# A fourth double-width raw weight tile in the wide layers of a two-layer encoder

## The chip, the cores and the metric

The kernel runs on one core of one Trainium2 chip. The metric is the time of one execution in microseconds (us), measured on the device; of several runs the median is taken. The core has five engines that matter here: TensorE (PE in the profile; PEld is its weight load), VectorE (DVE), ScalarE (ACT), GpSimd (POOL), and SyncE (SP), which here only issues transfers. Each engine works through its own queue in order and waits on semaphores that other engines and transfers raise.

## The reference

What is computed is the trunk of a bidirectional encoder with two layers over 512 tokens of width 1024, in float32:

```python
for layer in range(DEPTH):
    hn = rmsnorm(h, norm_mix[layer])
    if layer % 2 == 0:
        h = h + hybrid_attention(hn, ...)
    else:
        h = h + neighbourhood_attention(hn, ...)
    h = h + sq_relu_mlp(rmsnorm(h, norm_ffn[layer]), ffn_w_up[layer], ffn_w_down[layer])
return rmsnorm(h, final_norm)

def sq_relu_mlp(h, w_up, w_down):
    u = jax.nn.relu(h @ w_up)
    return (u * u) @ w_down
```

`w_up` is 1024 x 4096 and `w_down` 4096 x 1024. Layer 0 has 16 heads of full attention over the 512 tokens, layer 1 has 16 heads of attention over a window.

## The kernel before

Activations lie transposed (features on partitions, tokens along the free dimension). Every product is made in three matmuls from split operands: a value is its rounded high half (`hi`, made by ACT) and the rest (`lo`, made by DVE as value minus `hi`); high x high, high x low and low x high are summed in PSUM.

The MLP of each layer (`mlp_swept`) has four parts. First 6 tiles of 128 hidden features are made by plain products (`plain`), and their share of the second product is added. Then comes the **wide stage**, 26 more tiles in 13 blocks of 256 features: here a product of 2 x 2 tiles is made from seven block products instead of eight (`Seven`, in the manner of Strassen and Winograd), which needs sums of weight blocks. Then the **sweeps** multiply 22 of these tiles by `w_down` in the same manner in three kinds of passes of 11 steps, with weight sums prepared beforehand in DRAM (`SumsAhead`, transfers issued by ACT and POOL, L819 and L828). The last 4 tiles are plain again.

In the wide stage a block has 4 chunks (`seven_chunk`). Two chunks share one **raw pair**, a tile of 128 x 2048 floats from `raw_pair`: two transfers of 256 KB by SP (L312) fill four of the eight blocks of each half, POOL makes the others in three operations (L315 to L317), ACT makes `hi` of a half (L322) and DVE `lo` (L323). A pair can be loaded anew when both halves have been split. There are three such tiles (`bufs=3`), and three `hi` and three `lo` tiles. A chunk is used by 21 matmuls of 128x256 (L402 to L404). After four chunks a block's four PSUM banks are emptied by ACT (L411) and DVE (L412 to L415), and `raw_evac` squares the relu on ACT (L1210, L1211).

`weights(i)` is called ahead of the matmuls of chunk i. It asks for the loads of all chunks up to i + LOAD, with LOAD = 5, and for the splits up to i + AHEAD, with AHEAD = 2. The same tiles and the same function serve every other weight in the kernel; `raw_half` gives out one half of a pair at a time, from the list `spare`.

The order of instructions on each engine is set by a planner when the kernel is built: the program's order is the priority, and an instruction that could start earlier by the planner's own costs is pulled forward. Only the attention of layer 1 has an order written out by hand (`fixed_order`), and single instructions are held in program order by `keep_in_program_order`. Dependences are found by the planner from the parts of a tile that each instruction touches.

The pool `pp` has five tiles of 128 x 512 floats. They hold the attentions' probabilities (`p`, written at L1061 and L1698), the accumulator of the norms' squares (`acc`, L547), and in the third kind of sweeps one operand of each step (`u`, split at L1376 and L1377). The pool `scp` has six scratch tiles of the same size.

In layer 0 the kernel also prepares bias rows for layer 1's attention (`bias_rows`, L1285 to L1305) by SP transfers and POOL copies while the MLP runs.

Of the kernel before, what the change touches and what calls it, by code (L numbers as in the profile page):

```python
# [8 lines left out]
F32 = mybir.dt.float32  # L9
F32R = mybir.dt.float32r  # L10
# [6 lines left out]
S = 512  # L17
D = 1024
P = 128
# [11 lines left out]
def f32(ap):  # L31
    return ap.bitcast(F32)
# [3 lines left out]
def encoder_kernel(ctx: ExitStack, tc: tile.TileContext, ins, out, dbg=None):  # L36
# [3 lines left out]
    big = ctx.enter_context(tc.tile_pool(name="big", bufs=1))  # L40
    wp = ctx.enter_context(tc.tile_pool(name="wp", bufs=3))
    scp = ctx.enter_context(tc.tile_pool(name="scp", bufs=6))
    pp = ctx.enter_context(tc.tile_pool(name="pp", bufs=5))
    tp = ctx.enter_context(tc.tile_pool(name="tp", bufs=6))
    ps = ctx.enter_context(tc.tile_pool(name="ps", bufs=1, space=PSUM))
    dr = ctx.enter_context(tc.tile_pool(name="dr", bufs=1, space=bass.MemoryType.DRAM))
# [14 lines left out]
    def nm(s):  # L61
        cnt[0] += 1
        return f"{s}_{cnt[0]}"
# [18 lines left out]
    def sbk():  # L82
        return bank("s", 2)

    def stb():
        return bank("t", 2)

    def ob():
        return bank("o", 1)

    def scratch(dt=F32):
        return scp.tile([P, 512], dt, tag="sc", name=nm("sc"))

    def tiny(n, dt=F32):
        return tp.tile([P, n], dt, tag=f"ti{n}", name=nm("ti"))

    def keep(shape, dt, name):
        return big.tile(shape, dt, tag=name, name=name)


    cst = keep([P, C_ROPE], F32, "cst")
    ident = cst[:, C_ID : C_ID + P]
# [78 lines left out]


    spare = []

    def raw_pair():
        return wp.tile([P, 2048], F32, tag="raw", bufs=3, name=nm("raw"))

    def raw_half():
# [50 lines left out]


    asked, loaded, ready, low_parts = [], [], [], []
    AHEAD, LOAD = 2, 5

    def plan(*spec, make=None):
        asked.append((make or chunk, spec))
        return len(asked) - 1

    def weights(i, ahead=AHEAD):
        while len(loaded) < min(i + LOAD + 1, len(asked)):
            make, spec = asked[len(loaded)]  # L250
            loaded.append(make(*spec))
            next(loaded[-1])
        while len(ready) < min(i + ahead + 1, len(asked)):
            hi, lo, lows = next(loaded[len(ready)])
            ready.append((hi, lo))
            low_parts.append(lows)

            give_low(len(ready) - fixed[0])
        give_low(i + 1)
        return ready[i]  # L260
# [4 lines left out]
    def give_low(n):  # L265
        while given[0] < n:
            for z in low_parts[given[0]]:
                z()
            given[0] += 1
# [247 lines left out]
    def tick(us):  # L517
        if beat["rest"]:
            return
        beat["left"] -= us  # L520
        if beat["left"] <= 0:
            beat["left"] += beat["every"]
            next(beat["work"], None)

    def drain():
        for _ in beat["work"]:
            pass
# [33 lines left out]


    X = [Slot() for _ in range(KD)]
    acc = pp.tile([P, S], F32, tag="p", name=nm("acc"))

    def make_x(k):
        b = stb()
# [453 lines left out]
    def attend(heads, step):  # L1021


        late_t, late_v = [], []

        def transpose(h, i, p):
            if i % 2 == 0:
                h["pt"] = Slot(), Slot()
            h3, l3 = (s_.t.rearrange("p (k q) -> p k q", k=4)[:, :, (i % 2) * P : (i % 2 + 1) * P] for s_ in h["pt"])
            tb = stb()  # L1030
            for k in range(4):
                PE.transpose(tb[:, k * P : (k + 1) * P], p[:, k * P : (k + 1) * P], ident)  # L1032
            t3 = tb.rearrange("p (k q) -> p k q", k=4)
            ACT.activation(h3, t3, AF.Copy)
            DVE.tensor_tensor(l3, t3, f32(h3), op=ALU.subtract)
            if i % 2:
                late_v.append((h, i // 2, h["pt"]))

        def values(h, half, pt):
            if half == 0:  # L1040
                h["o"] = ob()
            o = h["o"]
            for k in range(4):
                for n, m in enumerate(pt):
                    PE.matmul(o[:, 256 * half : 256 * half + 256], h["vlhs"](k), m.t[:, 256 * k : 256 * k + 256],  # L1045
                              start=k == 0 and n == 0, stop=k == 3 and n == 1, skip_group_check=True)
            for s_ in pt:
                s_.free()
            if half:
                fold(o, h["e"])  # L1050
                h["after"]()

        def scores(h, i):
            s = sbk()
            pl = h["passes"](i)
            for n, (lh, rh) in enumerate(pl):
                PE.matmul(s, lh, rh, start=n == 0, stop=n == len(pl) - 1)  # L1057
            h["done"](i)
            t = tiny(4)
            p = pp.tile([P, 512], F32, tag="p", name=nm("p"))  # L1060
            DVE.tensor_tensor_reduce(p, s, zeros.to_broadcast([P, S]), op0=ALU.add, op1=ALU.min, scale=h["scale"](i),  # L1061
                                     scalar=3e38, accum_out=t[:, 1:2])
            ACT.activation(p, p, AF.Exp, bias=t[:, 1:2], scale=-1.0, accum_out=t[:, 2:3])
            DVE.reciprocal(t[:, 3:4], t[:, 2:3])  # L1064
            POOL.tensor_scalar(p, p, t[:, 3:4], 1.0, op0=ALU.mult, op1=ALU.mult)  # L1065
            return p

        for h in heads:
            for i in range(4):
                ripe = list(late_v)  # L1070
                tick(1.3)
                p = scores(h, i)
                if len(late_t) == 3:
                    transpose(*late_t.pop(0))
                late_t.append((h, i, p))
                if ripe:
                    values(*late_v.pop(0))
                step(h, i)
        for x in late_t:
            transpose(*x)  # L1080
            while late_v:
                values(*late_v.pop(0))
            fill.run(1.5)
# [88 lines left out]
    def first_product(l):  # L1172

        w = ins["ffn_w_up"][l]
        X = [Slot() for _ in range(KD)]
        acc = pp.tile([P, S], F32, tag="p", name=nm("acc"))
        for k in range(KD):
            split_g(hT[:, k, :], gffn(l, k), X[k].pair())
            sumsq_acc(k, acc, DVE)
# [160 lines left out]
    class Sweeps:  # L1340
# [28 lines left out]
        def tokens(self, kind, kp):  # L1369

            r, s2 = self.parts(kp)
            two = Slot()
            d = two.t.rearrange("p (q z n) -> p q z n", q=2, z=2)

            def split_to(hi, lo, src):
                ACT.activation(hi, src, AF.Copy)  # L1376
                DVE.tensor_tensor(lo, src, f32(hi), op=ALU.subtract)  # L1377

            got = [d[:, 0], d[:, 1]]
            if kind == 0:  # L1380
                split_to(d[:, :, 0], d[:, :, 1], r[:, 0:4:2])
                self.one(kp)
                if kp < 2:
                    self.two(kp)
            elif kind == 1:
                for q, src in enumerate((r[:, 0], s2)):
                    split_to(d[:, q, 0], d[:, q, 1], src)
                if kp + 2 < self.n:
                    self.two(kp + 2)
                if kp + 2 >= self.n:  # L1390
                    self.three(kp + 2 - self.n)
                    self.four(kp + 2 - self.n)
            else:
                if kp + 2 < self.n:
                    self.three(kp + 2)
                    self.four(kp + 2)
                split_to(d[:, :, 0], d[:, :, 1], r[:, 1:3])
                one = pp.tile([P, 512], F32R, tag="p", name=nm("u"))
                e = one.rearrange("p (z n) -> p z n", z=2)
                split_to(e[:, 0], e[:, 1], r[:, 3])  # L1400
                got.append(e)
                self.R[kp].free()
                if kp % 4 == 3 or kp == self.n - 1:
                    self.second[kp // 4].free()
            return two, got
# [90 lines left out]

    def mlp_swept(l, made, last=None):

        stage, ahead, later = first_product(l)
        w = ins["ffn_w_down"][l]  # L1500
        bias = bias_rows() if l == 0 else iter(())
# [29 lines left out]

        rest = split_more()
        drain()
        reserve[0] = 6
        if last:
            beside = last(FIRST + RAW, V)
# [22 lines left out]


    X = [Slot() for _ in range(KD)]
    acc = pp.tile([P, S], F32, tag="p", name=nm("acc"))
    for k in range(KD):
        split_g(hT[:, k, :], gmix(1, k), X[k].pair())
    XP = [s_.pair() for s_ in X]
# [103 lines left out]
    def attend_C(step):  # L1669
# [18 lines left out]

        def scores(h, us):
            sb = sbk()  # L1690
            pt = pp.tile([P, 512], F32, tag="p", name=nm("p"))
            got = []
            for n, u in enumerate(us):
                unit(h, u, sb[:, 256 * n : 256 * n + 256], n == 0)
            for n, u in enumerate(us):
                tt = tiny(4)
                h[u] = pt[:, 256 * n : 256 * n + 256]
                DVE.tensor_tensor_reduce(h[u], sb[:, 256 * n : 256 * n + 256], h["bias"][:, 0 if u < 3 else 1, :],  # L1698
                                         op0=ALU.add, op1=ALU.min, scale=-1.0, scalar=3e38, accum_out=tt[:, 0:1])
                got.append((h[u], tt))  # L1700
            return got
# [290 lines left out]
```

## Time and profile before

| | us |
|---|---|
| median of 3 runs | 1185.34 |
| lowest and highest of them | 1185.12, 1186.34 |
| the profiled execution | 1187.7 |
| its span, first to last instruction | 1185.9 |
| wide stage of layer 0 | 338.4 to 476.3 |
| wide stage of layer 1 | 903.4 to 1039.2 |
| mean granted TensorE clock | 0.997 of full speed |

The page of the profile shows one execution. The groups of the wide stage in it are these (line, engine, operation, tiles, shapes and count; busy us and mean ns of one; idle time of the engine just before them and what ended most of it):

```profile
L323 DVE TENSOR_TENSOR wlo<-raw,whi 128x896 fp32r<-128x896 f32 x104 | 151.3, 1467 | 63.9 <-ACT whi L322 63.6
L322 ACT ACTIVATE whi<-raw 128x896 fp32r<-128x896 f32 x104 | 95.8, 946 | 98.7 <-POOL raw L317 44.7
L315 POOL TENSOR_TENSOR raw<-raw 128x256 f32<-128x256 f32 x52 | 56.0, 1078 | 76.3 <-DMA raw<-in_ffn_w_up_dram 56.4
L316 POOL TENSOR_TENSOR raw<-raw 128x512 f32<-128x512 f32 x52 | 83.1, 1599 | 4.1
L317 POOL TENSOR_TENSOR raw<-raw 128x256 f32<-128x256 f32 x52 | 68.0, 1308 | 4.1
```

Idle time of an engine that is not the bound costs nothing by itself; what counts is whether it reaches TensorE. A matmul's end is modelled, and matmuls overlap, so a matmul's busy time is longer than its share of the pipeline: the count of matmuls in a stretch says more than their busy time. A wait is put down to the engine whose signal came last.

### The profile page before, as it was taken

How to read it: one execution, taken by the hardware profiler on the slowest of the kernel's cores; microseconds unless marked ns; L12 is line 12 of the kernel's file. 1: busy time of each engine (PE TensorE's matmuls, PEld its weight loads, DVE VectorE, ACT ScalarE, POOL GpSimd, SP SyncE). 2: the span in 40 equal slices, each digit the busy share in tenths (PEclk: the TensorE clock that was granted, in tenths of full speed). 3: DMA queues.
4: the chain of work that ended last, by engine and by line, in shares of the span. 5: the costliest groups of instructions: out<-in, count | busy, mean ns of one | idle time of the engine just before them, and what ended most of it. 6: DMA issues, size and time to landing. Idle time of an engine off the chain costs nothing.

```text
span 1185.9 us, 20854 instructions
## 1 busy us (share of the span) xinstructions
PE 1152.0 (97%) x7596; PEld 1034.0 (87%) x7596; DVE 917.2 (77%) x1617; ACT 668.1 (56%) x1147; POOL 459.4 (39%) x486
## 2 busy tenths in 40 slices
PE   9989999999999999999999999999999999999997
PEld 8667778888899899999988998988889989999995
DVE  4788888778968777998474676767996777899855
ACT  5468576664535556756253565655553555576625
POOL 3267353333478795000001243333265878700000
PEclk9999999999999999999999999999999999999999
DMA  7123467654656666877345577778557666575702
GB/s 270 54 76 85 116 148 197 180 103 133 147 147 175 164 143 171 272 236 250 131 119 148 141 215 183 207 175 214 166 112 192 161 174 160 150 243 170 257 2 71
DMA packets 129543, 191.55 MB, mean 162 GB/s; under 512 B 12659, under 2 KB 81184, under 8 KB 128736
## 3 DMA queue, kind: packets, MB, share of 16 engines
q1 hardware_dynamic: 112304, 136.61, 36.8%
q0 software_dynamic: 14976, 29.38, 15.5%
q10 hardware_dynamic: 2160, 24.22, 6.3%
q8 instruction: 60, 0.98, 0.4%
q14 instruction: 43, 0.35, 0.1%
HBM read 167.75 MB, written 52.43 MB: 186 GB/s over the span
## 4 chain that ended last, share of the span: by engine, by line
PE 75%; DVE 10%; ACT 4%; DMA 4%; issue 3%; POOL 3%; SPq 0%; DVEq 0%; ACTq 0%; POOLq 0%
PE mm L531 7%; PE mm L533 7%; PE mm L532 7%; DVE wlo L323 3%; DMA raw<-in_ffn_w_up_dram 3%; PE s L1057 3%; PE t L1432 3%; PE t L1433 2%; PE t L1431 2%; PE o L1045 2%; PE t L1032 2%; PE mm L1433 2%; PE mm L1431 2%; PE mm L1432 2%; PE s L533 2%
## 5 line engine op out<-in xcount | busy, mean ns | idle before, releaser
L323 DVE TENSOR_TENSOR wlo<-raw,whi 128x896 fp32r<-128x896 f32 x104 | 151.3, 1467 | 63.9 <-ACT whi L322 63.6
L531 PE MATMUL mm<-a,whi 128*128 128x512 f32 x407 | 165.0, 407 | 0.3 <-ACT whi L223 0.2
L532 PE MATMUL mm<-a,whi 128*128 128x512 f32 x407 | 161.4, 396 | 0.1
L533 PE MATMUL mm<-a,wlo 128*128 128x512 f32 x407 | 160.4, 396 | 0.3 <-DVE wlo L213 0.3
L322 ACT ACTIVATE whi<-raw 128x896 fp32r<-128x896 f32 x104 | 95.8, 946 | 98.7 <-POOL raw L317 44.7
L223 ACT ACTIVATE whi<-raw 128x1024 fp32r<-128x1024 f32 (+3 forms) x94 | 88.9, 948 | 89.6 <-PE s L532 29.4
L213 DVE TENSOR_TENSOR wlo<-raw,whi 128x1024 fp32r<-128x1024 f32 (+4 forms) x91 | 105.8, 1165 | 37.0 <-ACT whi L223 36.9
L533 PEld LDWEIGHTS mm<-a,wlo 128*128 128x128 f32 x407 | 76.7, 189 | 17.4 <-DVE wlo L213 0.7
L531 PEld LDWEIGHTS mm<-a,whi 128*128 128x128 f32 x407 | 76.8, 189 | 16.2 <-issue 0.9
L532 PEld LDWEIGHTS mm<-a,whi 128*128 128x128 f32 x407 | 76.9, 189 | 14.0 <-DVE a L575 0.4
L315 POOL TENSOR_TENSOR raw<-raw 128x256 f32<-128x256 f32 x52 | 56.0, 1078 | 76.3 <-DMA raw<-in_ffn_w_up_dram 56.4
L316 POOL TENSOR_TENSOR raw<-raw 128x512 f32<-128x512 f32 x52 | 83.1, 1599 | 4.1
L404 PE MATMUL mm<-a,wlo 128*128 128x256 f32 x280 | 80.0, 286 | 3.1 <-DVE wlo L323 2.7
L1065 POOL TENSOR_SCALAR p<-p,ti 128x512 f32<-128x512 f32 x64 | 48.3, 758 | 86.3 <-DVE ti L1064 55.3
L1595 POOL DMA_DIRECT2D a<-a x16 | 8.7, 546 | 182.7 <-PE mm L532 167.9
L403 PE MATMUL mm<-a,whi 128*128 128x256 f32 x280 | 78.5, 280 | 0.0
L402 PE MATMUL mm<-a,whi 128*128 128x256 f32 x280 | 78.4, 280 | 0.0
L1432 PE MATMUL t<-a,whi 128*128 128x256 f32 x264 | 74.4, 282 | 2.1 <-DVE a L1377 2.1
L1431 PE MATMUL t<-a,whi 128*128 128x256 f32 x264 | 74.0, 280 | 0.0
L1433 PE MATMUL t<-a,wlo 128*128 128x256 f32 x264 | 73.9, 280 | 0.0
L1687 POOL TENSOR_SCALAR p<-p,ti 128x256 f32<-128x256 f32 x64 | 36.1, 574 | 97.2 <-DVE ti L1686 89.9
L317 POOL TENSOR_TENSOR raw<-raw 128x256 f32<-128x256 f32 x52 | 68.0, 1308 | 4.1
(390 smaller groups left out, 3878.3 us busy)
## 6 DMA issues: line engine op xcount, KB each, us to landing
raw<-in_ffn_w_up_dram SPq DMA_DIRECT2D x104, 256.0 KB
made<-in_ffn_w_down_dram ACTq DMA_DIRECT2D x44, 512.0 KB
a<-made SPq DMA_DIRECT2D x68, 256.0 KB
made<-in_ffn_w_down_dram POOLq DMA_DIRECT2D x44, 256.0 KB, 5.4
made<-made POOLq DMA_DIRECT2D x44, 256.0 KB, 6.0
raw<-in_ffn_w_down_dram SPq DMA_DIRECT2D x20, 512.0 KB
raw<-in_ffn_w_down_dram SPq DMA_DIRECT2D x40, 256.0 KB
raw<-in_od_w_qkv_dram SPq DMA_DIRECT2D x64, 128.0 KB
```

The lines of the kernel that those rows point to most:

```text
L213: z = lambda: (eng or DVE).tensor_tensor(to, src, f32(high), op=ALU.subtract)
L223: ACT.activation(hi[:, 0:m], raw[:, 0:m], AF.Copy)
L316: POOL.tensor_tensor(r[:, :, 4:6], r[:, :, 2:3].to_broadcast([P, n, 2, P]), r[:, :, 0:7:6], op=ALU.add)
L322: ACT.activation(hi[:, 0:896], raw[:, 128:1024], AF.Copy)
L323: DVE.tensor_tensor(lo[:, 0:896], raw[:, 128:1024], f32(hi[:, 0:896]), op=ALU.subtract)
L404: PE.matmul(o, wl, x[:, 0], start=False, stop=kp == self.np - 1, skip_group_check=True)
L531: PE.matmul(o, wh, xh, start=first, stop=False)
L532: PE.matmul(o, wh, xl, start=False, stop=False)
L533: PE.matmul(o, wl, xh, start=False, stop=last)
L1431: PE.matmul(o, wh, x[:, 0], start=first and m % 2 == 0, stop=False, skip_group_check=True)
L1432: PE.matmul(o, wh, x[:, 1], start=False, stop=False, skip_group_check=True)
L1433: PE.matmul(o, wl, x[:, 0], start=False, stop=last, skip_group_check=True)
```

## The change

The pool `pp` goes. In its place stands one tile `shared` of 128 x 2560 floats. The probabilities take its five parts of 512 in turn (`p_tile`), and `acc` is always its fifth part. While `wide[0]` is set, `raw_pair` gives `shared[:, 0:2048]` as every fourth pair, between three from the pool. `mlp_swept` sets this at its start, together with LOAD = 7, and takes both back at the drain after the wide stage, where it also empties `spare`. The operand `u` of the sweeps comes from the scratch tiles.

```diff
-    pp = ctx.enter_context(tc.tile_pool(name="pp", bufs=5))
...
+    shared = keep([P, 2560], F32, "shared")
+    turn_p = [0]
+
+    def p_tile():
+        turn_p[0] = (turn_p[0] + 1) % 5
+        return shared[:, 512 * turn_p[0] : 512 * turn_p[0] + 512]
+
+    acc = shared[:, 2048:2560]
...
     spare = []
+    wide = [0]
 
     def raw_pair():
+        if wide[0]:
+            wide[0] = wide[0] % 4 + 1
+            if wide[0] == 1:
+                return shared[:, 0:2048]
         return wp.tile([P, 2048], F32, tag="raw", bufs=3, name=nm("raw"))
...
-    AHEAD, LOAD = 2, 5
+    AHEAD = 2
+    LOAD = [5]
...
-        while len(loaded) < min(i + LOAD + 1, len(asked)):
+        while len(loaded) < min(i + LOAD[0] + 1, len(asked)):
...
-    acc = pp.tile([P, S], F32, tag="p", name=nm("acc"))
...
-            p = pp.tile([P, 512], F32, tag="p", name=nm("p"))
+            p = p_tile()
...
-                one = pp.tile([P, 512], F32R, tag="p", name=nm("u"))
+                one = scratch(F32R)
...
     def mlp_swept(l, made, last=None):
 
+        wide[0], LOAD[0] = 4, 7
         stage, ahead, later = first_product(l)
...
         rest = split_more()
         drain()
+        wide[0], LOAD[0] = 0, 5
+        spare.clear()
         reserve[0] = 6
...
-            pt = pp.tile([P, 512], F32, tag="p", name=nm("p"))
+            pt = p_tile()
```

The line that makes `acc` goes in all three places where it stood.

More of the change, by code (lines that the diff above doesn't have):

```diff
@@ L1175, in first_product @@
         X = [Slot() for _ in range(KD)]
-        acc = pp.tile([P, S], F32, tag="p", name=nm("acc"))
         for k in range(KD):
@@ L1561, in encoder_kernel @@
     X = [Slot() for _ in range(KD)]
-    acc = pp.tile([P, S], F32, tag="p", name=nm("acc"))
     for k in range(KD):
```

## The prediction

> **What bounds the kernel now.** First the page: who is busy.
>
> ```profile
> span 1185.9 us, 20854 instructions
> PE 1152.0 (97%) x7596; PEld 1034.0 (87%) x7596; DVE 917.2 (77%) x1617; ACT 668.1 (56%) x1147; POOL 459.4 (39%) x486
> ```
>
> TensorE (PE) is the bound; only time in which it waits can be won. Next the table by stretches for PE alone (length, busy time, instructions): the two wide stages (L402 to L404, one in each layer), a stretch of layer 0 without a wait, and then pieces of both stages.
>
> ```profile
> 338.35:476.35 138.00, 132.75 (x1093) 1.00 0.64 163
> 903.44:1039.30 135.86, 131.85 (x1093) 1.00 0.65 163
> 340.00:360.00 20.00, 20.00 (x170) 1.00 0.64 174
> 348.45:369.60 21.15, 20.50 (x170) 1.00 0.69 187
> 385.40:432.80 47.40, 43.78 (x354) 1.00 0.70 164
> 923.00:956.00 33.00, 31.20 (x259) 1.00 0.67 175
> 1000.10:1039.30 39.20, 38.55 (x324) 1.00 0.67 166
> 369.60:385.40 15.80, 15.78 (x132) 1.00 0.62 145
> 432.80:476.35 43.55, 42.59 (x355) 1.00 0.58 159
> 903.44:923.00 19.56, 19.56 (x167) 1.00 0.66 162
> 956.00:1000.10 44.10, 42.55 (x348) 1.00 0.63 151
> ```
>
> A matmul takes 20.00/170 = 0.1176 us where PE never waits, at a granted clock of 1.00. A wide stage has 13 blocks x 4 chunks x 21 = 1092 matmuls, so it could take 128.4 us. It takes 138.0 and 135.9: 9.6 + 7.4 = 17.0 us are lost, more than the idle shown, since matmul ends are modelled and overlap. This is the ceiling of the change. A chunk of 21 is 2.47 us, a raw pair (two chunks) 4.94 us.
>
> Then who waits for whom, in layer 0's wide stage (SyncE's queue, POOL, ACT, PE: total us, times, longest), and SyncE in layer 1's:
>
> ```profile
> SPq L312 <- DVE wlo L323: 93.8, 22, 8.4
> POOL raw L315 <- DMA raw<-in_ffn_w_up_dram: 17.5, 8, 6.9
> ACT whi L322 <- POOL raw L317: 23.0, 11, 4.6
> PE s L404 <- DVE wlo L323: 3.2, 5, 1.5
> SPq L312 <- DVE wlo L323: 93.3, 22, 5.7
> ```
>
> Read from the end: PE waits for the low half, ACT for POOL's sums, POOL for the transfer, and the transfer's issue for DVE to release the raw tile: 22 of the stage's 26 pairs, 4.3 us each. The chain of waits shows one such ring whole (start, us, what):
>
> ```profile
> 348.45 1.63 DVE wlo L323
> 350.14 0.37 SPq L312
> 350.56 5.79 DMA raw<-in_ffn_w_up_dram
> 356.50 0.76 POOL raw L315
> 357.33 2.02 POOL raw L316
> 359.44 1.47 POOL raw L317
> 360.93 0.96 ACT whi L322
> 361.92 2.24 DVE wlo L323
> ```
>
> From the release at 350.08 to the next low half at 364.16 are **14.1 us**. With three pairs, pair j waits for the last chunk of pair j-3, five chunks before its own first: 5 x 2.47 = 12.4 us. The ring is 1.7 us longer than what PE pays for it, so any reserve is used up and PE waits.
>
> **The change part by part.**
>
> *The fourth pair and LOAD 7.* Pair j now waits for pair j-4: seven chunks, 17.3 us, against a ring of 14.1 us: 3.2 us of slack where 1.7 us were short. No load, sum or split is added; 26 pairs per stage stay. By the chain, the first four pieces above behind the clean stretch hold such a ring, the last four do not. Their losses (length less 0.1176 x count) are 1.15 + 5.77 + 2.54 + 1.10 = **10.6 us** with a ring, and 0.28 + 1.80 - 0.08 + 3.18 = **5.2 us** without. (The remaining 1.2 us lie in instructions counted on both sides of a cut and the first 10 us.)
>
> What is late next when the ring is slack: the hi and lo tiles, still three, so that a split cannot start before PE leaves the chunk three back; the relu and square at L1210 and L1211; and the port that DVE and POOL seem to share. I take these from the pieces without a ring: 5.2 us lost on (132 + 355 + 167 + 348) x 0.1176 = 117.8 us of matmuls, 4.4%. The ring's pieces have 1107 x 0.1176 = 130.2 us of matmuls. At 4.4% they would still lose 5.7 us, so the gain is 10.6 - 5.7 = 4.9 us; if their waits vanish whole, 10.6 us. Part of the 5.2 us is itself the tail of a ring just before (432.8 follows one, 956 too), so neither end is nearer: I take the middle, **-7.7 us**, and keep both ends.
>
> *Where the loads and sums move.* Loads go up to one pair, 4.94 us, earlier on SyncE's queue; behind a waiting load stand other loads and, in layer 0, the bias rows (L1285 to L1305), which nothing reads before layer 1's attention. The sums move ahead of DMA issues on POOL (L819); these feed the sweeps' second kind, and the first kind alone has 11 chunks x 24 matmuls x 0.1176 = 31 us after the stage's end. Cost 0, hidden by those 31 us.
>
> *The first loads of the sweeps* (L1319) are asked seven ahead too, and a leftover half is dropped at the drain. PE's waits after the stages are for tokens, not for loads, the second row being layer 1's:
>
> ```profile
> PE t L1432 <- DVE a L1377: 0.7, 1, 0.7
> PE t L1432 <- DVE a L1377: 1.4, 2, 1.0
> ```
>
> Cost 0; bounds: -1.4 us if DVE arrives with less behind it, +1.4 us if these waits double.
>
> *Probabilities, acc and u.* The probabilities keep five tiles of 512, now in a fixed ring; no instruction is added. The one row in which a probability waits for its tile, and the two of the u splits in layer 0's wide stage:
>
> ```profile
> DVE p L1061 <- PE t L1032: 1.6, 2, 1.0
> L1376 ACT ACTIVATE u<-a x5: 398/402/405, 357.6 to 401.6; 128x256 fp32r<-128x256 f32 x5
> L1377 DVE TENSOR_TENSOR u<-a,u x5: 412/420/1523, 360.8 to 402.8; 128x256 fp32r<-128x256 f32 x5
> ```
>
> The p wait may double or go: -1.6 to +1.6 us, and I take 0, since the depth is the same. acc (L547) is written when the last probabilities have long been read: 0. The planner pulled five u splits forward into the stage, as many as there were p tiles; with six scratch tiles it can pull six: one more 0.42 us on DVE and 0.40 on ACT in each stage, beside matmuls; 0, or 0.8 us in both stages if DVE has no cover.
>
> **Sum**: 1187.7 us (profiled execution: span 1185.9 and 1.8 around it) - 7.7 = 1180.0 us. That execution was 2.4 us over the median of the runs shown, 1185.34; by that, **1177.6 us**.
>
> **A rule that speaks against it.** Shortest, median and longest ns of the four operations of the pair in layer 0's stage, and four operations in their order from POOL's and DVE's timelines:
>
> ```profile
> L323 DVE TENSOR_TENSOR wlo<-raw,whi x50: 1077/1487/2236, 339.4 to 470.9; 128x896 fp32r<-128x896 f32 x50
> L315 POOL TENSOR_TENSOR raw<-raw x24: 726/971/2262, 341.8 to 461.8; 128x256 f32<-128x256 f32 x24
> L316 POOL TENSOR_TENSOR raw<-raw x24: 1274/1300/2142, 342.7 to 463.5; 128x512 f32<-128x512 f32 x24
> L317 POOL TENSOR_TENSOR raw<-raw x24: 737/1464/1567, 344.8 to 464.9; 128x256 f32<-128x256 f32 x24
> ```
>
> ```profile
> 996.27 1.30 POOL L316 TENSOR_TENSOR raw<-raw 128x512 f32<-128x512 f32 x1
> 997.65 1.46 POOL L317 TENSOR_TENSOR raw<-raw 128x256 f32<-128x256 f32 x1
> ...
> 996.51 3.55 DVE L323 TENSOR_TENSOR wlo<-raw,whi 128x896 fp32r<-128x896 f32 x2 [1.62 <-ACT whi L322]
> ```
>
> The four at 996.27 end at 1000.06, after 3.79 us; their shortest times add to 1.27 + 0.74 + 2 x 1.08 = 4.16 us. They ran in turn, with a tenth of it overlapped. The Trainium skill, "SBUF — State Buffer", section "SBUF: two separate sides", says that a VectorE operation with two SBUF inputs and a GpSimd operation that reads SBUF take one port pair as an exclusive lock; these rows agree.
>
> Rival 1 is this as a bound. A pair's port work is 2 x 1.077 + 0.726 + 1.274 + 0.737 = 4.89 us against PE's 4.94. In layer 0's stage it is 50 x 1.077 + 24 x 2.737 + 5 x 0.41 = 121.6 of 138.0 us, 88%. If 88% is all that two queues in order can reach, the fourth tile only moves one sum per stage ahead of it: 2.74/0.88 = 3.1 us. Were that reached in one layer alone, the gain is 3.1 us: **1182.2 us** (6.2 us and 1179.1 in both). For it: the losses without a ring. Against: by 3.79 to 4.16 the true work is 4.89 x 0.91 = 4.45 us a pair, and PE had 20.00 of 20 us at 340 with the sums running.
>
> **Other rivals.** *2, the tile doesn't help*: the planner keeps its order, or SyncE is held elsewhere. For it, this row ahead of layer 0's stage:
>
> ```profile
> SPq L1296 <- POOL a L1292: 14.9, 1, 14.9
> ```
>
> A bias row held the queue for 14.9 us with loads behind it. Against: inside the stage L312 waits for nothing but DVE's release. Time: **1185.3 us**, 1.5 either way.
>
> *3, the whole loss goes*: 17.0 us, **1168.3 us**; it needs the pieces without a ring to be only a ring's tail.
>
> *4, slower*: sums that are ready sooner take the port just before the low half that PE needs next. DVE is busy 104.9 us in layer 0's stage:
>
> ```profile
> 338.35:476.35 138.00, 132.75 (x1093) 129.87 (x1092) 104.90 (x107) 77.95 (x96) 104.38 (x90) 1.00 0.64 163
> ```
>
> Of these 73.2 us are the 50 low halves (their sum by line), 1.46 us each. With a mean of X the stage needs 31.7 + 50 X on DVE; this passes today's 138.0 at X = 2.13. At the longest seen, 2.236, it is 143.5 us: 5.5 us more, 11 in both layers, **1196.3 us**. Against: POOL does no more work than before, and a release 4.94 us early leaves the low half time to be hit.
>
> **How the numbers follow.** A gain or loss under 0.2% (2.4 us, about what a measurement of this kernel can tell from no change) counts as the same: 1183.0 to 1187.7. Forecast (gain 4.9 to 10.6, with the small bounds 1174 to 1181): 0.48. Rival 1: 0.19, a fifth of it under 2.4 us. Rival 2: 0.16, all of it the same. Rival 3: 0.07. Rival 4: 0.10. Faster is 0.48 + 0.15 + 0.07 = 0.70; same 0.04 + 0.16 = 0.20; slower 0.10. The range takes in rivals 1 and 2 and reaches nearly to 3: **1169.0 to 1186.0**, leaving out rival 4 and the upper edge of rival 2 above, and the lower half of rival 3.
>
> **What would show it.** Right: SyncE's waits for L323 shrink or their loads land before POOL asks (L315 waiting for the transfer falls from 17.5 us to under 5); no DMA in the chain of waits inside the stages; stages of about 134 and 132 us. Wrong: low halves longer than 1.5 us in the mean and PE still late (rivals 1 and 4); unchanged waits of POOL for the transfer (rival 2); or a loss in the attentions, where nothing but the tiles' place changed. It would also be wrong if the sweeps after the stages gave the gain back on DVE.

## The result and the profile after

| | before | after |
|---|---|---|
| median of the runs, us | 1185.84 | 1172.65 |
| lowest and highest, us | 1185.12, 1186.37 | 1171.78, 1173.18 |
| the profiled execution, us | 1187.7 | 1173.18 |
| its span, us | 1185.9 | 1171.4 |

The median before is now that of four runs. The ratio is 0.9888, with a 95% interval of 0.9871 to 0.9906: 13.2 us or 1.1% faster. The forecast was 1177.6 us, in a range of 1169.0 to 1186.0.

These are the first lines of the profile's page after the change. The new file is 12 to 14 lines longer there: L404 is now L418, L323 is L337, L322 is L336, L312 is L326 and L315 to L317 are L329 to L331.

```profile
span 1171.4 us, 20855 instructions
PE 1144.9 (98%) x7596; PEld 1029.6 (88%) x7596; DVE 919.4 (78%) x1617; ACT 668.2 (57%) x1147; POOL 463.6 (40%) x486
```

The engines do the same work; what went is time in which TensorE waited. The table by stretches gives the two wide stages after the change (length, TensorE's busy time and instructions, clock, transfers):

```profile
336.45:467.43 130.98, 129.96 (x1093) 1.00 0.67 169
895.53:1026.15 130.62, 129.57 (x1093) 1.00 0.68 172
```

They were 138.0 and 135.9 us: **7.0 and 5.3 us shorter, 12.3 us together**. Over the floor of 128.4 us, 2.6 and 2.2 us are left. The waits in layer 0's stage, those that stood in the prediction (SyncE's queue, POOL, then ACT and TensorE):

```profile
SPq L326 <- DVE wlo L337: 87.7, 26, 6.6
POOL raw L329 <- DMA raw<-in_ffn_w_up_dram: 7.4, 4, 3.9
ACT whi L336 <- PE s L417: 13.7, 9, 2.2
ACT whi L336 <- PE o L417: 8.5, 6, 1.8
PE mm L418 <- DVE wlo L337: 0.5, 1, 0.5
PE s L418 <- DVE wlo L337: 0.4, 1, 0.4
```

SyncE still waits for DVE's releases, 26 times and nearly as long as before: it loads as far ahead as the tiles allow, with three tiles or four. The wait one step on tells the two kernels apart: POOL's for the transfer fell from 17.5 to 7.4 us, and ACT's wait for POOL's sums (23.0 us before) has no row any more. Layer 1's stage shows the same: POOL's wait fell from 27.8 to 9.2 us, ACT's for the last of the sums from 21.7 to 1.3. ACT's splits now wait mostly for TensorE to give back a hi tile, 22.2 us in the two rows above. The same two rows before the change came to half of that:

```profile
ACT whi L322 <- PE s L403: 6.2, 4, 1.8
ACT whi L322 <- PE o L403: 4.8, 4, 1.5
```

The two spans differ by 14.5 us. For the rest of it, each stretch is measured between the starts of the first and last matmuls of its stages. The sweeps took 110.4 and 111.3 us before, 110.0 and 109.9 after. The stretch from the last scores of layer 0 to its wide stage took 96.2 us before and 97.0 after, that from the last scores of layer 1 to its wide stage 92.5 before and **94.5 after**: 0.8 and 2.0 us longer. The attention of layer 1 was 0.5 us shorter, and the stretches up to the end of layer 0's scores 2.7 us shorter. The last of these is scatter: the kernels with the change end there at 239.5 to 243.1 us, and runs whose code is alike up to there lie 3 us apart.

### The profile page after: what moved, and what is told of

Read it like the earlier page. It is cut to its first block, busy times and chain, and to the rows that moved or that the text cites. A ratio compares the mean times of both kernels' runs of the same rounds, so it can differ in the third digit from the quotient of the medians.

```text
span 1171.4 us, 20855 instructions
## 1 busy us (share of the span) xinstructions
PE 1144.9 (98%) x7596; PEld 1029.6 (88%) x7596; DVE 919.4 (78%) x1617; ACT 668.2 (57%) x1147; POOL 463.6 (40%) x486
## 4 chain that ended last, share of the span: by engine, by line
PE 79%; DVE 10%; DMA 4%; ACT 3%; issue 2%; POOL 1%; SPq 0%; DVEq 0%; POOLq 0%; ACTq 0%
PE mm L547 7%; PE mm L545 7%; PE mm L546 7%; PE t L1444 3%; PE t L1443 2%; PE t L1445 2%; PE mm L418 2%; PE mm L416 2%; PE mm L417 2%; PE s L1070 2%; PE o L1058 2%; PE mm L1445 2%; PE mm L1443 2%; PE mm L1444 2%; PE t L1045 2%
## 5 line engine op out<-in xcount | busy, mean ns | idle before, releaser
L337 DVE TENSOR_TENSOR wlo<-raw,whi 128x896 fp32r<-128x896 f32 x80 | 110.5, 1388 | 28.6 <-ACT whi L336 28.4
L236 ACT ACTIVATE whi<-raw 128x1024 fp32r<-128x1024 f32 (+3 forms) x86 | 80.4, 939 | 86.4 <-PE s L546 29.7
L226 DVE TENSOR_TENSOR wlo<-raw,whi 128x1024 fp32r<-128x1024 f32 (+4 forms) x83 | 99.2, 1197 | 36.1 <-ACT whi L236 34.4
L336 ACT ACTIVATE whi<-raw 128x896 fp32r<-128x896 f32 x80 | 75.4, 949 | 83.6 <-PE o L546 22.9
L546 PEld LDWEIGHTS mm<-a,whi 128*128 128x128 f32 x407 | 76.8, 189 | 14.1 <-DVE a L903 0.4
L1078 POOL TENSOR_SCALAR shared<-shared,ti 128x512 f32<-128x512 f32 x64 | 48.3, 758 | 84.5 <-DVE ti L1077 53.5
L418 PE MATMUL mm<-a,wlo 128*128 128x256 f32 x280 | 78.8, 282 | 0.7 <-DVE wlo L337 0.7
L1701 POOL TENSOR_SCALAR shared<-shared,ti 128x256 f32<-128x256 f32 x64 | 35.5, 566 | 95.9 <-DVE ti L1700 83.6
L330 POOL TENSOR_TENSOR raw<-raw 128x512 f32<-128x512 f32 x40 | 67.8, 1695 | 3.1
L1341 DVE TENSOR_TENSOR wlo<-a,whi 128x1024 fp32r<-128x1024 f32 x42 | 51.1, 1221 | 19.4 <-ACT whi L1340 19.4
L329 POOL TENSOR_TENSOR raw<-raw 128x256 f32<-128x256 f32 x40 | 45.1, 1127 | 44.0 <-DMA raw<-in_ffn_w_up_dram 26.1
```

Source lines behind the costliest of these rows:

```text
L226: z = lambda: (eng or DVE).tensor_tensor(to, src, f32(high), op=ALU.subtract)
L236: ACT.activation(hi[:, 0:m], raw[:, 0:m], AF.Copy)
L337: DVE.tensor_tensor(lo[:, 0:896], raw[:, 128:1024], f32(hi[:, 0:896]), op=ALU.subtract)
L418: PE.matmul(o, wl, x[:, 0], start=False, stop=kp == self.np - 1, skip_group_check=True)
L546: PE.matmul(o, wh, xl, start=False, stop=False)
```

## The experiments

Theory R: the round of a raw pair (release, load, sums, split) had no reserve with three pairs, and the fourth pair gives it one. Rivals: L, that asking seven chunks ahead does it; M, that the new places of the probabilities, `acc` and `u` do it; P, the port that DVE and POOL seem to share. Ratios are to the kernel before, run on the same chip; the wide stages are measured as above, in one profile each.

| run | edit to the kernel after | median us | ratio, 95% interval | wide stages us |
|---|---|---|---|---|
| e1 | loads asked five ahead | 1175.45 | 0.9902 [0.9885, 0.9919] | 131.7, 131.4 |
| e2 | no fourth pair, six ahead | 1188.69 | 1.0022 [1.001, 1.0034] | 139.2, 135.7 |
| e3 | no fourth pair, five ahead | 1186.75 | 1.0006 [0.9992, 1.002] | 138.0, 135.2 |
| e4 | fourth pair in layer 0 alone | 1179.46 | 0.9942 [0.9926, 0.9958] | 130.9, 136.0 |
| e5 | and a fourth hi and lo tile | 1169.58 | 0.987 [0.9851, 0.9888] | 129.1, 128.2 |
| e6 | shared pair last in turn | 1172.78 | 0.9897 [0.9879, 0.9915] | 131.2, 130.7 |
| e7 | e5 and e6 | 1168.61 | 0.9852 [0.9833, 0.9871] | 129.1, 128.2 |
| e8 | three pairs, six ahead, four hi and lo tiles | 1189.4 | 1.0037 [1.0022, 1.0053] | 138.8, 135.2 |
| e9 | none | 1173.15 | 0.989 [0.9869, 0.9911] | 131.0, 131.2 |
| e10 | e6 again | 1171.31 | 0.9866 [0.9849, 0.9884] | 131.1, 131.3 |
| e11 | shared pair every third time | 1175.59 | 0.9901 [0.9878, 0.9923] | 133.6, 132.7 |
| e12 | shared pair every second time | 1217.32 | one run | 147.6, 151.3 |

### Which part does it: e1 to e4

In e1, e2, e3 and e4 only the line that turns the fourth pair and the deeper asking on is edited. The excerpt shows its four versions one below the other, with the run's label added:

```diff
-        wide[0], LOAD[0] = 4, 7
+        wide[0], LOAD[0] = 4, 5                                  # e1
+        wide[0], LOAD[0] = 0, 6                                  # e2
+        wide[0], LOAD[0] = 0, 5                                  # e3
+        wide[0], LOAD[0] = (4, 7) if l == 0 else (0, 5)          # e4
```

> The changed kernel with loads asked five chunks ahead again, the fourth pair kept. Theory R (the ring: release, load, sums, split; the fourth pair alone makes it slack, and the planner pulls loads forward by itself): 1171 to 1175 us, both wide stages at 130 to 132 us. Rival L (the deeper asking does it): near the kernel before, 1182 to 1186 us, wide stages 136 to 138 us.

> The changed kernel without the fourth pair, loads asked six chunks ahead, which is the most that three pairs allow. Theory R: wide stages stay at 135 to 138 us; in all 1181 to 1185 us, what is under 1185 coming from outside the wide stages. Rival L: most of the gain, 1174 to 1177 us.

> Only the new place of the probabilities, acc and u; three pairs, loads five ahead. Theory R: wide stages 135 to 138 us, 1181 to 1185 us; the 3.2 us that the changed kernel won in the two attentions and the 1.9 us in the sweeps show here if they come from the new places, so 1181 to 1183 us if they do and 1185 if they do not. Rival M (the new places do most of it): under 1177 us.

> The fourth pair and the seven chunks in layer 0 alone. Theory R: layer 0's wide stage 131 us as in the changed kernel, layer 1's 135 to 136 us as before, in all 1177 to 1179 us. Rivals L and M do not tell; if the two layers' gains were not additive, 1173 or 1183 us.

Measured: e1 keeps the gain without the deeper asking, e2 has the deeper asking and no gain (it is 0.2% slower, and 1188.69 lies beyond what either theory said), e3 is no different from before, and e4 has layer 0's share. The medians of e1, e3 and e4 lie 0.5, 1.8 and 0.5 us above theory R's ranges; the wide stages lie within them. So it is the fourth pair. The planner pulls a load forward as soon as a tile is free, whatever the order asked in; from five to seven ahead, the stages shrink by 0.8 us each in one profile and the ratios overlap. The gains of the layers add: in e4 one wide stage is that of the kernel after, the other that of before. The table by stretches of e4 and e2:

```profile
338.82:469.67 130.85, 130.25 (x1093) 1.00 0.69 176
895.41:1031.45 136.04, 132.25 (x1093) 1.00 0.64 160
```

```profile
339.36:478.59 139.23, 133.31 (x1093) 1.00 0.62 160
905.66:1041.34 135.68, 132.21 (x1093) 1.00 0.64 161
```

e3 also bears on the 3.2 us that the kernel after showed in the attentions and the 1.9 us in the sweeps: the new places alone bring nothing that can be measured.

### What is late next, and the port: e5, e7, e8

e5 takes two free slots as a fourth hi and lo tile for every fourth chunk, and asks for splits three chunks ahead:

```diff
+    extra, turn_s = [], [0]
...
-        hi = wp.tile([P, 1024], F32R, tag="whi", name=nm("whi"))
-        lo = wp.tile([P, 1024], F32R, tag="wlo", name=nm("wlo"))
+        turn_s[0] = turn_s[0] % 4 + 1
+        if extra and turn_s[0] == 4:
+            hi, lo = (s_.t for s_ in extra)
+        else:
+            hi = wp.tile([P, 1024], F32R, tag="whi", name=nm("whi"))
+            lo = wp.tile([P, 1024], F32R, tag="wlo", name=nm("wlo"))
...
-                hi, lo = weights(ids[kp])
+                hi, lo = weights(ids[kp], 3 if extra else AHEAD)
...
         reserve[0] = 3
         sweeps = []
+        extra[:] = [Slot(), Slot()]
...
+        for s_ in extra:
+            s_.free()
+        extra.clear()
```

> The changed kernel with a fourth hi and a fourth lo tile in the wide stages, from two slots that are free there, and splits asked three chunks ahead. Theory R: with four pairs the ring is slack and ACT's split waits for TensorE to give a hi tile back; a fourth one takes most of what is left over 128.4 us: wide stages from 130.9 and 130.5 to 129 to 130 us, in all 1170 to 1172 us. Rival P (the port that DVE and POOL share is what is left): no change, 1172 to 1174 us, or slower if the low halves meet more sums.

The stages fall to the floor, and TensorE is busy for the whole of both:

```profile
339.10:468.20 129.10, 129.10 (x1093) 1.00 0.67 168
895.16:1023.40 128.24, 128.24 (x1093) 1.00 0.69 175
```

The median is 1169.58 us, 0.4 us below what was expected. Over the whole kernel this step is not clear of the scatter: the ratios of e5 and of the kernel after have intervals that overlap. The stages are what shows it. Rival P falls as a bound: with the same sums, the same number of low halves and the same two engines, TensorE has no idle time left in either stage.

e8 is e5 without the fourth pair (`wide[0], LOAD[0] = 0, 6`).

> Three pairs, loads six ahead, but four hi and lo tiles. Theory R: a split can come one chunk earlier and gives the raw pair back 2.5 us earlier, so the ring has 14.8 us for its 14.1: about half to three quarters of the wide stages' gain, 131 to 135 us each, 1175 to 1182 us in all. Rival (only the number of raw pairs counts): as with three pairs, 1185 to 1189 us.

This expectation of R failed and the rival's held: 1189.4 us, and no gain in either stage. ACT's waits in layer 0's stage show why, first in e8 and then in e2, which also has three pairs and loads six ahead, but no spare hi and lo tile:

```profile
ACT whi L342 <- POOL raw L333: 47.1, 21, 4.1
```

```profile
ACT whi L336 <- POOL raw L331: 27.6, 13, 4.4
```

With a hi tile to spare ACT still stands waiting for the sums, and longer. Splits cannot come earlier than their raw data, so nothing is released earlier. Here the two reserves were not exchangeable: raw pairs first, then hi and lo tiles.

### A cost that the prediction missed: e6, e7, e9, e10

The 2.0 us lost ahead of layer 1's wide stage lie at the start of its MLP. This is the chain of waits of the kernel after there (start, us, what):

```profile
807.82 16.77 DMA shared<-in_ffn_w_up_dram
824.70 1.07 ACT whi L236
825.79 1.23 DVE wlo L226
```

And SyncE's waits there:

```profile
SPq L214 <- DVE wlo L226: 14.1, 4, 8.2
SPq L214 <- PE t L1723: 7.5, 2, 7.3
```

The shared pair comes first in turn, so the MLP's second chunk lands in the third and fourth part of the probabilities, which the attention's last transposes (L1723) still read. Its load is issued only at 807.82, behind four others, and lands 16.8 us later; the low half is late and matmuls wait. e6 lets the turn begin at one (`wide[0], LOAD[0] = 1, 7`), so that the shared pair is the fourth.

> The changed kernel with the shared pair as the fourth in turn and not the first. Theory R2: the 2.0 us that layer 1's plain stage lost come from the second half of the shared pair, which waits for the last probabilities' transposes and lands behind four other loads; then that stage is back at 92.5 us from 94.5 and the whole at 1170 to 1171.5 us. Rival: the loss comes from asking seven chunks ahead, and stays: 1172 to 1174 us.

> Both of the two edits before. If they add: 1168 to 1170 us. If the wide stage is at its floor by the port: as the second alone.

In e6, e7 and e10 that stretch is 92.4 to 92.6 us, as before the change (92.5). But e6's median, 1172.78 us, was not below the kernel after's, run on another occasion, and lies in the rival's range. So both ran again, side by side:

> The changed kernel as it is, beside the next run on the same chip: 1172 to 1174 us, layer 1's plain stage 94 to 95 us.

> The shared pair as the fourth in turn, again, beside the changed kernel on the same chip. Theory R2 (the wait for the last probabilities costs 2.8 us in the two plain stages, and the first trial's total hid it under the scatter of the attention): 1.5 to 3 us below the changed kernel. Rival (the shorter plain stage is given back elsewhere): no difference.

e10 is 1.8 us below e9, and the intervals overlap. e9's stretch was not the expected 94 to 95 us but 92.7: its shared load waited for the transposes about as long, but ACT split it 15.2 us after its issue and not 16.9. Over all profiles the stretch is 94.5 us (the kernel after), 94.1 (e1), 93.5 (e5), 92.7 (e9) and 94.5 (e11) where the shared pair comes first, and 92.3 to 92.6 in the eight without it or with it last; e12, at 98.6, uses it every second time. So the late load is real, and the turn removes it. It cost between 0.2 and 2.0 us in this stretch. In layer 0's, 97.0 us in the kernel after, e4 and e5 stand against 96.0 in e1 and e9 and 96.2 before, so up to 0.8 us more. What it costs a whole run on average these runs don't settle. **e7 has both edits and the lowest median here**: 0.9852 of the kernel before, a further 0.4% below the kernel after by the two ratios, whose intervals just touch.

### Is it a rate, or a reserve: e11 and e12

A round that takes 16 us and three tiles would pass a pair every 5.3 us against TensorE's 4.94, and 26 x 5.3 = 138 us is layer 0's stage. Two issues of SyncE into the same tile, before the change (the timeline, three pairs apart), are 16.6 us from one another (16.3 in the mean of both stages):

```profile
350.14 0.37 SPq L312 DMA_DIRECT2D raw<-in_ffn_w_up_dram  x1
...
366.72 0.37 SPq L312 DMA_DIRECT2D raw<-in_ffn_w_up_dram  x1
```

But this sum comes out whatever the cause: where every tile is loaded again as soon as it is free, the time from one load of a tile to its next is the number of tiles times the pace of the pairs. With four tiles it should then be about four times 5.04 us, and so it is. The loads of the shared tile in the kernel after follow each other in 20.8 us in the mean of layer 0's stage:

```profile
344.17 2.29 SPq L326 DMA_DIRECT2D shared<-in_ffn_w_up_dram  x2
...
363.86 2.79 SPq L326 DMA_DIRECT2D shared<-in_ffn_w_up_dram  x2
...
386.22 1.92 SPq L326 DMA_DIRECT2D shared<-in_ffn_w_up_dram  x2
```

To test whether a round can be shorter, the four tiles stay, but the shared one is used more often than the others:

```diff
-            wide[0] = wide[0] % 4 + 1
+            wide[0] = wide[0] % 3 + 1          # e11; e12: % 2
...
-        wide[0], LOAD[0] = 4, 7
+        wide[0], LOAD[0] = 3, 6            # e11; e12: 2, 4
```

In both, a shared pair is loaded anew before it has been split, so a part of a product is made from other weights. In e11 it is the wide stage's first (in layer 0 loaded at 268.6 us, over weights that ACT splits at 302.7), in e12 one of the plain tiles' (from 245.5 us on three loads go into its two halves before the first split at 262.6). The instructions are the same in number and size.

> Four raw pairs in memory as in the changed kernel, but the shared one comes every third time (loads six ahead, as its turn then needs). Theory R, as a rate: a pair's round from load to release takes about 16 us; a tile that comes every third time lets a pair pass every 16/3 = 5.3 us, whatever the others do, so 26 pairs take 136 to 140 us as before and the whole 1184 to 1189 us. Rival (four tiles in memory are enough, or the port is what counts): wide stages 131 us, 1172 to 1175 us.

> The same with the shared pair every second time, loads four ahead. Theory R, as a rate: 16/2 = 8 us a pair, 26 pairs less the two that are loaded ahead: wide stages of 190 to 208 us, the whole 1290 to 1327 us. Rival: as the changed kernel.

Both expectations of the rate failed; both runs' stages lie between them and the rival's. With a tile that must go round within three pairs, e11 lost 5.2 and 4.3 us over the floor, about half of what the kernel before loses. The granted clock was 0.99 in the first of these stages, by which 128.4 us alone become 129.7 (an estimate). In e12, one run, it was 0.97 and 0.99, against 1.00 in most other stages. Its loads of the shared tile in layer 0's stage (the timeline of SyncE) follow each other in 10.3 to 13.5 us, 11.4 in the mean:

```profile
361.82 1.43 SPq L326 DMA_DIRECT2D shared<-in_ffn_w_up_dram  x2
367.91 1.03 SPq L326 DMA_DIRECT2D raw<-in_ffn_w_up_dram  x2
375.33 3.33 SPq L326 DMA_DIRECT2D shared<-in_ffn_w_up_dram  x2
382.78 0.88 SPq L326 DMA_DIRECT2D raw<-in_ffn_w_up_dram  x2
386.87 3.35 SPq L326 DMA_DIRECT2D shared<-in_ffn_w_up_dram  x2
```

So a pair can go round in 11.4 us where TensorE waits for that tile; 13 such rounds fill the stage's 147.6 us. Three tiles with rounds of 11.4 us would pass a pair every 3.8 us (an estimate), well under the 4.94 that TensorE needs. The three tiles of the kernel before are thus not a fixed rate but too small a reserve: of a round of 16.6 us, some 5 us are waiting (the difference to 11.4, an estimate). Where this waiting lies, in the queues of POOL, ACT or DVE, was not separated.

## Why the prediction was right, and where not

**The bound and the ceiling** held. 17.0 us were said to be all that could be won in the wide stages; e5 and e7 reach 129.1 and 128.2 us where 128.4 was worked out.

**The fourth pair** held as the mechanism: e1 has the gain with it alone, e2 and e3 have none without it. The row on which it rested, SyncE waiting for DVE's release, was the right place but a poor gauge: it hardly moved (93.8 to 87.7 us). The row behind it, POOL waiting for the transfer, moved as said, if not under the 5 us named (7.4). Another sign, no DMA in the chain of waits inside the stages, did not come: one round is still in layer 0's chain, in the stretch where most of that stage's remaining loss lies (start, us, what):

```profile
393.74 7.52 DMA raw<-in_ffn_w_up_dram
```

**The mis-sized term** is the step "At 4.4% they would still lose 5.7 us", and the middle of 7.7 us taken from it. The wide stages gave 12.3 us, more than the 10.6 of the upper end; the whole kernel's 13.2 us left 1172.65, below the forecast's own 1174 to 1181, and inside the stated range only because that was drawn to take in rivals too. The order of the 1092 matmuls of a stage is the same in both kernels, so the same pieces can be followed. These are the rows after the change, first the four pieces with a ring, then the four without:

```profile
346.62:366.46 19.84, 19.84 (x171) 1.00 0.66 172
382.06:425.32 43.26, 42.34 (x354) 1.00 0.68 160
915.15:945.50 30.35, 30.35 (x260) 1.00 0.68 186
988.18:1026.09 37.91, 37.91 (x323) 1.00 0.70 186
366.46:382.06 15.60, 15.60 (x134) 1.00 0.76 184
425.32:467.37 42.05, 41.95 (x355) 1.00 0.63 179
895.55:915.15 19.60, 19.60 (x167) 1.00 0.63 142
945.50:988.18 42.68, 41.63 (x350) 1.00 0.69 164
```

Counted from the start of a piece's first matmul to the start of the next piece's first, so that none counts twice, the pieces with a ring lost 11.7 us before and 2.2 after. That is 1.7% of their matmuls' 130 us, not 4.4%. The pieces without a ring lost 5.2 us before and 2.5 after: about half of that was a tail of a late pair just ahead. The prediction named such tails, but left these pieces out of the gain and took their rate for the others.

**The ring's sum** (14.1 us against 5 x 2.47 = 12.4) had the right sign and the wrong form. It took releases to be paced by TensorE; in e8 a spare hi and lo tile brought no release forward, since ACT waited for the sums. And the round is elastic: 11.4 us in e12, 16.6 before, 20.8 with four tiles.

**Costs put at nothing**: for the probabilities, `acc` and `u` this was right (e3, ratio 1.0006). For the first loads of the stage it was missed: the prediction looked at the probabilities waiting for tiles, and not at loads waiting for probabilities. That wait is in the profile; the two stretches ahead of the wide stages were 2.0 and 0.8 us longer in it. The sweeps gained 0.5 and 1.4 us in the profile instead of giving anything back, 1.9 us where 1.4 were allowed; that DVE comes to them with less behind it would fit, but was not tested by itself.

**The rivals.** Rival 1, the port at 88%, falls with e5: by the rival's own sum of shortest times, 121.6 us, the port is busy for 94% of its 129.1 us (an estimate). Rival 4, slower, is refuted by the result. Its low halves hardly changed: their sum in layer 0's stage is 71.85 us after and was 73.2 before, 1.44 us each where it was 1.46, far from the 2.13 that the rival needs. Those that read pool tiles became shorter (a median of 1487 ns before), those that read the shared tile did not:

```profile
L337 DVE TENSOR_TENSOR wlo<-raw,whi x38: 1081/1151/2178, 337.5 to 461.8; 128x896 fp32r<-128x896 f32 x38
L337 DVE TENSOR_TENSOR wlo<-shared,whi x12: 1091/1612/2183, 342.5 to 447.7; 128x896 fp32r<-128x896 f32 x12
336.45:467.40 130.95, 71.85 (x50) 1.00 0.67 169
```

Rival 2 is refuted by the result, and rival 3, the whole 17.0 us, took a second edit: e5's stages give 16.5 of it.

## What to carry to other kernels

Where a loader waits for a buffer at every turn, look one step on: only if its consumer waits for the data is the buffer short. Here one more buffer then won most of the loss, tails included. Buffers of successive steps were not exchangeable; add them in the order in which the waits name them, and run again, since the next short one shows only then. Memory borrowed from another phase is free only where its old readers are done: here the first load into it came late, and putting it last in turn took the plain stage back to its old length.

## What was not expected of the hardware

A pair went from one load of its tile to the next in 11.4 us in e12, where TensorE waited for that tile, in 16.6 us in the kernel before and in 20.8 us in the kernel after, with the same transfer of 512 KB and the same operations. How much of the difference between the first two is the order of the queues, and how much DVE and POOL taking turns as in the prediction's rows, was not separated: low halves lasted from 1.08 to 2.19 us in e5's layer 0, and yet TensorE had no idle time in its wide stages.
